# A feed-forward output layer: one 512-column matmul in place of two of 256 columns

## The chip, the cores and the metric

The kernel runs on one core of one Trainium2 chip. The metric is the device time of one execution of the whole program in microseconds (us): two layers of a small model on a sequence of 256 tokens.

## What is computed

The model has two layers. Each layer is a mixer (a state-space branch and an attention branch, merged) and a feed-forward part with a short convolution, and each of them adds its result to the running activations `x`. The change lies in the second matrix product of the feed-forward part:

```python
def conv_ffn(h, w_in, conv_w, conv_b, w_out):
    a, b = jnp.split(h @ w_in, 2, axis=-1)
    a = lax.conv_general_dilated(a, conv_w[:, None, :], window_strides=(1,),
                                 padding=[(CONV_WIDTH - 1, 0)], ...) + conv_b
    return (jax.nn.gelu(a) * b) @ w_out

for l in range(DEPTH):                       # 2 layers, 256 tokens, D_MODEL 1024, D_FF 2816
    x = x + hybrid_mixer(rmsnorm(x, norm_mix[l]), ...)
    x = x + conv_ffn(rmsnorm(x, norm_ffn[l]), ...)
return rmsnorm(x, norm_final)
```

All of it is float32 in the reference.

## The kernel before

Activations lie transposed, features on the 128 partitions and the 256 tokens (`T`) along the free dimension. `w_out` is then 8 output blocks `m` of 128 features, each the sum of 22 products `k` (`KD` = 8, `NF` = 22), so 176 products a layer.

Most products are done in three matmuls, so that the fast matmul type fp32r keeps float32 accuracy. A weight chunk of 1024 columns (8 tiles of 128x128) is loaded into a ring of five `raw` buffers (L147, DMAs on the SP queue). `split` (L154) makes two parts of it: ScalarE casts `raw` to the high part `wh` (L158) and VectorE subtracts it for the low part `wl` (L160); `wh` and `wl` have three buffers each, so a cast waits until TensorE has used the chunk three before. The activations are split in the same way, into `fh` and `fl` here (`split_act`, L163). `mm3` (L167) then issues wh·fh, wh·fl and wl·fh (L169, L170, L171), 256 columns each, all into the first half of one PSUM bank; every matmul loads its own 128x128 weights first (PEld in the profile).

In the output loop of `ffn` (from L944) a block `m` takes a bank `ps_fo` of the two banks with the tag `mm`, runs its 22 products and is then added to `x` by VectorE (`tt`, an addition that the profile shows as L204). Block m+2 needs the bank of block m, and so waits for that addition. Each chunk holds 8 products and is split just ahead of its use, whatever block it falls into: chunk `fo5` is products 40 to 47, `fo6` begins with product 48. In layer 0 the loop also prepares layer 1: after some blocks further chunks are loaded and split (`pre`, L182), and the matrix C of the state-space branch is scaled (`ctmp`, `Cm`).

Nobody writes the order of the instructions by hand in this stage. The program is built with a scheduler that simulates a time line (L1174) and puts every engine's instructions in the order in which that simulation finds them ready; only some rows of TensorE in the mixers are kept together (L175). A changed instruction can therefore move others far behind it. Names in the profile that the text uses: `ps_g` are gate products in the mixer, `pr` and `z` the state-space branch's element-wise products and scans, `rt` and `sw` the rotary embedding, `kk` the compressed keys, `ps_n`, `sq`, `xo` and `ps_x` the final normalization and transposition.

## Time and profile before

| | before |
|---|---|
| median of 3 runs | 856.54 us (854.37 to 856.77) |
| the profiled execution, its own time | 856.18 us |
| its span, first to last instruction | 854.4 us |
| TensorE busy | 813.5 us (95%) |
| VectorE busy | 677.5 us (79%) |
| ScalarE busy | 418.4 us (49%) |
| mean granted TensorE clock | 0.977 |

All times within the execution are counted from the start of the span. The output loop of layer 0 lies at 372 to 434 us, that of layer 1 at 783 to 844 us. The busy time of TensorE counts overlapping matmuls once; a matmul that is listed with 0.28 us can begin 0.11 us after the one ahead of it. For the cost of one matmul, read the distance of the starts.

### The profile page before, as it was taken

How to read it: one execution, taken by the hardware profiler on the slowest of the kernel's cores; microseconds unless marked ns; L12 is line 12 of the kernel's file. 1: busy time of each engine (PE TensorE's matmuls, PEld its weight loads, DVE VectorE, ACT ScalarE, POOL GpSimd, SP SyncE). 2: the span in 40 equal slices, each digit the busy share in tenths (PEclk: the TensorE clock that was granted, in tenths of full speed). 3: DMA queues.
4: the chain of work that ended last, by engine and by line, in shares of the span. 5: the costliest groups of instructions: out<-in, count | busy, mean ns of one | idle time of the engine just before them, and what ended most of it. 6: DMA issues, size and time to landing. Idle time of an engine off the chain costs nothing.

```text
span 854.4 us, 16283 instructions
## 1 busy us (share of the span) xinstructions
PE 813.5 (95%) x6432; PEld 738.4 (86%) x6432; DVE 677.5 (79%) x1277; ACT 418.4 (49%) x786; POOL 23.0 (3%) x56
## 2 busy tenths in 40 slices
PE   8997999999989999999989769999999999999996
PEld 7875786669989999999989657877799999999996
DVE  7979886747998988877666998988588888888553
ACT  3011244664544766656533126667546556655442
POOL 0000000000000000000001110100000000000000
PEclk9998989999999999999999979999999999999998
DMA  7545722625655666667753563234356566555641
GB/s 290 163 117 167 266 75 78 188 80 154 185 158 170 197 198 192 192 185 233 261 173 110 166 221 121 75 92 153 102 173 192 179 195 199 191 195 188 196 147 50
DMA packets 41772, 142.42 MB, mean 167 GB/s; under 512 B 5216, under 2 KB 6752, under 8 KB 41696
## 3 DMA queue, kind: packets, MB, share of 16 engines
q1 hardware_dynamic: 39712, 139.15, 51.1%
q10 hardware_dynamic: 1984, 2.24, 0.9%
q8 instruction: 50, 0.82, 0.4%
q14 instruction: 26, 0.21, 0.1%
HBM read 136.39 MB, written 2.10 MB: 162 GB/s over the span
## 4 chain that ended last, share of the span: by engine, by line
PE 75%; DVE 14%; DMA 5%; issue 3%; ACT 1%; POOL 0%; DVEq 0%; ACTq 0%; SPq 0%
PE ps_f L170 9%; PE ps_f L169 9%; PE ps_f L171 9%; PE ps_g L425 4%; PE ps_fo L171 3%; PE ps_fo L170 3%; PE ps_fo L169 3%; DMA raw<-wst 2%; DVE z L586 2%; PE ps_g L171 2%; PE ps_g L170 2%; PE ps_g L169 2%; PE psy L621 2%; DVE pr L204 2%; PE ps_br L169 2%
## 5 line engine op out<-in xcount | busy, mean ns | idle before, releaser
L158 ACT CAST wh<-raw 128x1024 fp32r<-128x1024 f32 (+1 forms) x199 | 207.6, 1046 | 225.4 <-PE ps_f L170 96.9
L160 DVE TENSOR_TENSOR wl<-raw,wh 128x1024 fp32r<-128x1024 f32 (+1 forms) x199 | 243.8, 1227 | 68.1 <-ACT wh L158 65.1
L170 PE MATMUL ps_f<-al,wh 128*128 128x256 f32 x704 | 195.2, 277 | 2.4 <-DVE al L213 2.4
L169 PE MATMUL ps_f<-ah,wh 128*128 128x256 f32 x704 | 195.3, 278 | 1.2 <-DVE x L213 1.2
L171 PE MATMUL ps_f<-ah,wl 128*128 128x256 f32 x704 | 194.9, 277 | 0.0
L170 PEld LDWEIGHTS ps_f<-al,wh 128*128 128x128 f32 x704 | 132.9, 189 | 2.6 <-DVE al L213 2.6
L169 PEld LDWEIGHTS ps_f<-ah,wh 128*128 128x128 f32 x704 | 132.9, 189 | 1.3 <-ACT wh L158 1.3
L171 PEld LDWEIGHTS ps_f<-ah,wl 128*128 128x128 f32 x704 | 132.8, 189 | 0.0
L171 PE MATMUL ps_fo<-fh,wl 128*128 128x256 f32 x352 | 96.9, 276 | 1.1 <-DVE wl L160 1.1
L170 PE MATMUL ps_fo<-fl,wh 128*128 128x256 f32 x352 | 97.0, 276 | 0.0
L169 PE MATMUL ps_fo<-fh,wh 128*128 128x256 f32 x352 | 96.9, 276 | 0.0
L171 PEld LDWEIGHTS ps_fo<-fh,wl 128*128 128x128 f32 x352 | 65.9, 188 | 1.3 <-DVE wl L160 1.3
L169 PEld LDWEIGHTS ps_fo<-fh,wh 128*128 128x128 f32 x352 | 66.1, 188 | 0.0
L170 PEld LDWEIGHTS ps_fo<-fl,wh 128*128 128x128 f32 x352 | 66.1, 188 | 0.0
L425 PE MATMUL ps_g<-xg,raw 128*128 128x256 f32 x256 | 64.2, 401 | 2.0 <-DMA raw<-wst 1.1
L425 PEld LDWEIGHTS ps_g<-xg,raw 128*128 128x128 f32 x256 | 49.0, 200 | 13.2 <-issue 4.1
L204 DVE TENSOR_TENSOR pr<-z,E 128x512 f32<-128x512 f32 x64 | 43.2, 720 | 8.5 <-PE psy L621 8.5
L169 PE MATMUL ps_g<-ah,wh 128*128 128x256 f32 x128 | 40.0, 312 | 4.4 <-ACT wh L158 4.4
L213 DVE SCALAR_TENSOR_TENSOR cv<-ab,sp,cv 128x255 f32<-128x255 f32 (+1 forms) x88 | 42.0, 480 | 1.7 <-ACT cv L926 0.4
L171 PE MATMUL ps_g<-ah,wl 128*128 128x256 f32 x128 | 39.7, 310 | 3.4 <-DVE wl L160 3.3
L586 DVE TENSOR_TENSOR_SCAN z<-rm,z 128x512 f32<-128x512 f32 x32 | 37.7, 1210 | 2.7 <-POOL z L204 2.7
L170 PE MATMUL ps_g<-al,wh 128*128 128x256 f32 x128 | 39.5, 308 | 0.0
(261 smaller groups left out, 1676.9 us busy)
## 6 DMA issues: line engine op xcount, KB each, us to landing
raw<-wst SPq DMA_DIRECT2D x246, 512.0 KB, 4.2
x<-xT SPq DMA_DIRECT2D x4, 512.0 KB, 4.9
raw<-wst SPq DMA_DIRECT2D x4, 420.0 KB, 3.6
B<-wst SPq DMA_DIRECT2D x2, 512.0 KB, 6.2
xd<-x SPq DMA_DIRECT2D x2, 512.0 KB, 6.6
x<-xd SPq DMA_DIRECT2D x2, 512.0 KB, 5.8
sw<-rt SPq DMA_DIRECT2D x12, 64.0 KB, 3.6
sw<-rt ACTq DMA_DIRECT2D x12, 64.0 KB, 3.8
```

What stands on the lines that cost most here:

```text
L158: S.copy(h[:, :n], t[:, :n])
L160: V.tensor_tensor(lo[:, :n], t[:, :n], h.bitcast(F32)[:, :n], op=OP.subtract)
L169: PE.matmul(ps, wh, ah, start=start, stop=False, **k)
L170: PE.matmul(ps, wh, al, start=False, stop=False, **k)
L171: PE.matmul(ps, wl, ah, start=False, stop=stop, **k)
L204: return e.tensor_tensor(o, a, b, op=op)
L213: e.scalar_tensor_tensor(o, a, s, b, op0=op0, op1=op1)
L425: PE.matmul(ps, w[:, k * 128:(k + 1) * 128], xg[:, k, :], start=k == 0, stop=k == KD - 1, skip_group_check=True)
L586: V.tensor_tensor_scan(f, rt.rearrange("p a t -> p (a t)"), f, 0.0, op0=OP.mult, op1=OP.add)
L621: PE.matmul(psy[32 * a:32 * a + 32, :T], Cm[:, ci, 4 * q + a, :], prs[a // 2][:, a % 2].rearrange("p c t -> p (c t)"), start=(i == 0), sto ...
```

## The change

`fh` and `fl` become the two halves of one tile `f2`, at the same addresses. The matmuls wh·fh and wh·fl become one matmul of 512 columns (L952 of the changed kernel) that writes both halves of the bank: the first half is the sum of the high parts, the second that of the low parts. The third matmul, wl·fh (L953), goes into the first half as before. Each block therefore needs two additions to `x` instead of one. Over both layers 1056 weight loads and matmuls become 704, and 16 additions of 128x256 are new.

```diff
--- before.py
+++ after.py
@@ -914,8 +914,7 @@
 
     def ffn(l, nm, mp):
         ah, al, x = nm.ah, nm.al, nm.x
-        fh = mp.tile([128, NF, T], F32R, name="fh")
-        fl = mp.tile([128, NF, T], F32R, name="fl")
+        f2 = mp.tile([128, 2, NF, T], F32R, name="f2")
         cw = [sp(l, f"cw{i}") for i in range(3)]
         cb = sp(l, "cb")
 
@@ -928,7 +927,7 @@
             stt(cv[:, 2:], ab[:, 0, :T - 2], cw[0][:, i:i + 1], cv[:, 2:], OP.mult, OP.add)
             S.activation(cv, cv, AF.Gelu_apprx_tanh)
             tt(cv, cv, ab[:, 1, :], OP.mult)
-            split_act(fh[:, i, :], fl[:, i, :], cv)
+            split_act(f2[:, 0, i, :], f2[:, 1, i, :], cv)
 
         for i in range(NF):
             ps = bank("ps_f", "mm" if i % 2 == 0 else "aux").rearrange("p (a t) -> p a t", a=2)
@@ -949,8 +948,11 @@
                 if t % 8 == 0:
                     c = split(l, f"fo{t // 8}")
                 wh, wl = wt(c, t % 8)
-                mm3(ps[:, :T], wh, wl, fh[:, k, :], fl[:, k, :], k == 0, k == NF - 1)
+
+                PE.matmul(ps, wh, f2[:, :, k, :], start=k == 0, stop=k == NF - 1, skip_group_check=True)
+                PE.matmul(ps[:, :T], wl, f2[:, 0, k, :], start=False, stop=k == NF - 1, skip_group_check=True)
             ix = tt(x[:, m, :], ps[:, :T], x[:, m, :], OP.add)
+            tt(x[:, m, :], ps[:, T:], x[:, m, :], OP.add)
             if m == 0:
                 first_out = ix
             if l + 1 < L:
```

The order of the instructions moves at three places that matter below. The first is TensorE in layer 1, at the last product (k = 21) of block m = 0; `ps_fo_9316` (before) and `ps_fo_9146` (after) are the bank of m = 0, `ps_fo_9405` and `ps_fo_9214` that of m = 1, and `wh_9379`/`wh_9193` is chunk `fo2`. Before:

```order
L170 MATMUL ps_fo_9405<-fl_7725,wh_9414 128x256
L171 MATMUL ps_fo_9405<-fh_7724,wl_9416 128x256
L169 MATMUL ps_fo_9405<-fh_7724,wh_9414 128x256
L170 MATMUL ps_fo_9316<-fl_7725,wh_9379 128x256
L171 MATMUL ps_fo_9316<-fh_7724,wl_9381 128x256
L170 MATMUL ps_fo_9405<-fl_7725,wh_9414 128x256
L171 MATMUL ps_fo_9405<-fh_7724,wl_9416 128x256
```

And with the change:

```order
L952 MATMUL ps_fo_9214<-f2_7555,wh_9243 128x512
L953 MATMUL ps_fo_9214<-f2_7555,wl_9245 128x256
L952 MATMUL ps_fo_9214<-f2_7555,wh_9243 128x512
L952 MATMUL ps_fo_9146<-f2_7555,wh_9193 128x512
L953 MATMUL ps_fo_9146<-f2_7555,wl_9195 128x256
L953 MATMUL ps_fo_9214<-f2_7555,wl_9245 128x256
L952 MATMUL ps_fo_9214<-f2_7555,wh_9243 128x512
```

The product's matmul with the low activations has to wait for VectorE's last `fl` (`f2`) split and is put into block m = 1. Before, its high half ran earlier and its other two matmuls stand behind 92 matmuls of the loop, some 31 products; now all of it stands behind 67 matmuls, 34 of 512 columns and 33 of 256. Layer 0 has the same rows.

The second place is VectorE there, from the last `fl` split on. `wl_9476`/`wl_9267` is the low part of chunk `fo5`, `wl_9512`/`wl_9296` of `fo6`. Before:

```order
L160 TENSOR_TENSOR wl_9446<-raw_9442,wh_9444 128x1024
L165 TENSOR_TENSOR fl_7725<-cv_9307,fh_7724 128x256
L204 TENSOR_TENSOR x_7420<-ps_fo_9316,x_7420 128x256
L160 TENSOR_TENSOR wl_9476<-raw_9472,wh_9474 128x1024
L160 TENSOR_TENSOR wl_9512<-raw_9508,wh_9510 128x1024
L160 TENSOR_TENSOR wl_9542<-raw_9538,wh_9540 128x1024
L204 TENSOR_TENSOR x_7420<-ps_fo_9405,x_7420 128x256
```

And with the change:

```order
L165 TENSOR_TENSOR f2_7555<-cv_9137,f2_7555 128x256
L160 TENSOR_TENSOR wl_9267<-raw_9263,wh_9265 128x1024
L204 TENSOR_TENSOR x_7251<-ps_fo_9146,x_7251 128x256
L160 TENSOR_TENSOR wl_9296<-raw_9292,wh_9294 128x1024
L204 TENSOR_TENSOR x_7251<-ps_fo_9146,x_7251 128x256
L160 TENSOR_TENSOR wl_9318<-raw_9314,wh_9316 128x1024
L204 TENSOR_TENSOR x_7251<-ps_fo_9214,x_7251 128x256 x2
```

The addition of block 0 stood ahead of the split of `fo5`. Now its first half stands behind that split, and its second half behind the split of `fo6` as well.

The third place is VectorE in the mixer of layer 1, which the diff doesn't touch. `wl_5742`/`wl_5573` and `wl_5901`/`wl_5732` are the low parts of two weight chunks for `ps_g`. Before:

```order
L586 SCALAR_TENSOR_TENSOR z_5330<-rm_5327,z_5330 128x512 x2
L204 TENSOR_TENSOR pr_5966<-z_5330,E_4228 128x512
L204 TENSOR_TENSOR pr_5968<-z_5330,E_4228 128x512
L204 TENSOR_TENSOR pr_5977<-z_5330,E_4228 128x512
L204 TENSOR_TENSOR pr_5979<-z_5330,E_4228 128x512
L204 TENSOR_TENSOR rt_5348<-rt_5348,rc_5041 128x512
L160 TENSOR_TENSOR wl_5901<-raw_5897,wh_5899 128x1024
L165 TENSOR_TENSOR y_5689<-yg_5687,y_5689 128x256
L204 TENSOR_TENSOR rt_5348<-rt_5348,sw_5410 128x512
```

And with the change:

```order
L586 SCALAR_TENSOR_TENSOR z_5161<-rm_5158,z_5161 128x512 x2
L204 TENSOR_TENSOR rt_5179<-rt_5179,rc_4872 128x512
L165 TENSOR_TENSOR y_5520<-yg_5518,y_5520 128x256
L204 TENSOR_TENSOR rt_5179<-rt_5179,sw_5241 128x512
L586 SCALAR_TENSOR_TENSOR z_5161<-rm_5158,z_5161 128x512 x2
L160 TENSOR_TENSOR wl_5732<-raw_5728,wh_5730 128x1024
L204 TENSOR_TENSOR pr_5797<-z_5161,E_4206 128x512
L204 TENSOR_TENSOR pr_5799<-z_5161,E_4206 128x512
L165 TENSOR_TENSOR q_4935<-rt_5179,q_4935 128x512
L204 TENSOR_TENSOR pr_5808<-z_5161,E_4206 128x512
L204 TENSOR_TENSOR pr_5810<-z_5161,E_4206 128x512
```

The split `wl_5901` stood behind four `pr` products and one `rt` step; now it stands ahead of the four products, and behind a second `rt` step and one `y` step that followed it before. A few rows ahead of these, four other `pr` products and the two `kk` products have moved ahead of the first split, `wl_5742`. From VectorE's next `th` step on the order is almost that of before.

## Rows read from the trace of the kernel before

**Rows 1.** The profile page: span, and busy time, share and instructions of each engine.

```profile
span 854.4 us, 16283 instructions
...
PE 813.5 (95%) x6432; PEld 738.4 (86%) x6432; DVE 677.5 (79%) x1277; ACT 418.4 (49%) x786; POOL 23.0 (3%) x56
```

**Rows 2.** Stages: window, length, then busy us of PE, PEld, DVE, ACT, POOL; PEclk, DMA.

```profile
372.00:434.00 62.00, 60.90 (x536) 60.71 (x536) 45.50 (x64) 33.62 (x48) 0.00 (x0) 1.00 0.71 230
...
540.00:550.00 10.00, 10.00 (x69) 8.58 (x67) 10.00 (x21) 5.48 (x16) 2.66 (x6) 0.83 0.17 54
783.00:844.00 61.00, 61.00 (x541) 61.00 (x540) 32.51 (x42) 27.55 (x38) 0.00 (x0) 1.00 0.44 142
```

**Rows 3.** Timeline of PE, layer 1: start us, us, engine, line, operation, count.

```profile
783.66 0.28 PE L169 MATMUL ps_fo<-fh,wh 128*128 128x256 f32 x1
...
794.31 0.28 PE L170 MATMUL ps_fo<-fl,wh 128*128 128x256 f32 x1
```

**Rows 4.** Timeline of all engines at the end of layer 1 and of the program.

```profile
843.39 0.28 PE L171 MATMUL ps_fo<-fh,wl 128*128 128x256 f32 x1
...
843.70 0.42 DVE L204 TENSOR_TENSOR x<-ps_fo,x 128x256 f32<-128x256 f32 x1 [5.59 <-PE ps_fo L171]
...
844.22 0.42 ACT L367 ACTIVATE sq<-x 128x256 f32<-128x256 f32 x1 [6.66 <-DVE x L204]
844.54 0.49 ACT L972 ACTIVATE xo<-x,sp 128x256 f32<-128x256 f32 x1
845.32 0.53 PEld L387 LDWEIGHTS ps_n<-ones,sq 128*128 128x128 f32 x4
...
845.68 0.29 PEld L1003 LDWEIGHTS ps_x<-cc,xo 128*128 128x128 f32 x2
```

**Rows 5.** Timeline of PE: the two-pass matmuls of an early stage.

```profile
23.68 6.42 PE L425 MATMUL ps_q<-xg,raw 128*128 128x256 f32 x29
29.94 1.24 PE L425 MATMUL ps_kc<-xg,raw 128*128 128x256 f32 x5
```

**Rows 6.** Timeline of PE: single-pass matmuls of 280 columns.

```profile
487.83 0.29 PE L171 MATMUL ps_v<-wh,al 128*128 128x280 f32 x1
...
488.23 0.29 PE L171 MATMUL ps_v<-wh,al 128*128 128x280 f32 x1
```

**Rows 7.** Timeline of ACT, layer 1, after the first output block.

```profile
794.40 2.00 ACT L158 CAST wh<-raw 128x1024 fp32r<-128x1024 f32 x2 [3.86 <-PE ps_fo L170]
```

**Rows 8.** Timeline of DVE, layer 1, at the same place.

```profile
794.51 0.42 DVE L204 TENSOR_TENSOR x<-ps_fo,x 128x256 f32<-128x256 f32 x1 [2.68 <-PE ps_fo L171]
795.48 2.37 DVE L160 TENSOR_TENSOR wl<-raw,wh 128x1024 fp32r<-128x1024 f32 x2 [0.55 <-ACT wh L158]
```

**Rows 9.** The chain that ended last, layer 0: start us, us, what.

```profile
388.45 1.06 ACT wh L158
...
393.94 4.81 DMA raw<-wst
...
402.15 6.34 DMA raw<-wst
...
427.93 0.39 PE ps_fo L171
```

**Rows 10.** Timeline of DVE in the mixer of layer 1.

```profile
502.90 3.96 DVE L204 TENSOR_TENSOR pr<-z,E 128x512 f32<-128x512 f32 x4
506.78 0.68 DVE L204 TENSOR_TENSOR rt<-rt,rc 128x512 f32<-128x512 f32 x1
507.39 1.21 DVE L160 TENSOR_TENSOR wl<-raw,wh 128x1024 fp32r<-128x1024 f32 x1
508.52 0.41 DVE L165 TENSOR_TENSOR y<-yg,y 128x256 fp32r<-128x256 f32 x1
508.86 0.68 DVE L204 TENSOR_TENSOR rt<-rt,sw 128x512 f32<-128x512 f32 x1
```

**Rows 11.** Timeline of PE at the same place.

```profile
508.65 0.58 PE L171 MATMUL ps_g<-ah,wl 128*128 128x256 f32 x1 [3.33 <-DVE wl L160]
```

## Prediction

> **What bounds the kernel now.** I read the page first: TensorE (PE) is busy for 813.5 of 854.4 us [rows 1], so the first guess is that every nanosecond taken from a matmul shortens the program. Busy time doesn't say that PE sets the end everywhere, so I read the two changed stages apart [rows 2]. Layer 1's output loop is PE alone: 61.00 of 61 us, with VectorE (DVE) at 32.51. Layer 0's loop looks almost the same, 60.90 of 62, but the chain that ended last leaves PE there: from the cast at 388.45 to the matmul at 427.93 it runs over casts, splits and the weight transfers of 4.81 and 6.34 us and others like them [rows 9]. What PE saves inside that stretch is waited away at its end. Third, I looked outside the stages: the scheduler has reordered the mixer of layer 1, and there PE waits 3.33 us for one weight split [rows 11].
>
> **The matmuls.** The 528 matmuls of layer 1's loop start from 783.66 to 843.39 [rows 3, 4]: 59.73 us over 527 distances, 0.1133 us each, 0.340 for a product of three. The change puts one 512-column matmul for two of 256. No row shows one of this type with all 128 rows, so I bound it. Below: the L425 matmuls are done in two passes, which stream 512 columns for one weight load, and 29 of them start within 6.26 us (23.68 to 29.94), 0.216 each [rows 5]. Above: fp32r matmuls of 280 columns start 0.133 apart (three distances from 487.83 to 488.23 [rows 6]), 0.476 ns a column, and 512 columns at that rate are 0.244. I take 0.216, since that row streams the same number of columns behind the same 128x128 load; the 280-column row has an odd width. A product is then 0.216 + 0.113 = 0.329, 0.011 less than 0.340; at the upper bound it is 0.357, 0.017 more. Over 176 products that is -1.9 us, or +3.0.
>
> The rule against this gain stands in the Trainium skill, "TensorE: Matmul & The Clock Gate", section "Back-to-back issue gap": a warm isolated matmul costs N/2.4 + 2.5 ns, so 216 ns for 512 columns but 109 for 256. By it a product would go from 327.5 to 325 ns and layer 1 would gain 0.4 us instead of 1.9, with 855.1 us in all instead of 853.6. On 512 columns the trace agrees with the page (0.216), on 256 it measures 113 and not 109, and the measurement decides.
>
> **Two new waits at the first block's end.** The last product of block 0 now stands as a whole behind 34 matmuls of 512 and 33 of 256 columns: 34 x 0.216 + 33 x 0.113 = 11.07 us, against 92 x 0.1133 = 10.42 before, so 0.65 later. On it hangs the buffer for chunk fo5. Before, its L170 started at 794.31 [rows 3], the cast of fo5 began at 794.40 and two casts took 2.00 [rows 7], and the two splits began at 795.48 and took 2.37, 1.18 each [rows 8]. Now the cast begins at about 795.15 (0.65, and 0.1 for the longer matmul), fo5's split at 796.23, and it ends at 797.41. PE reaches the first matmul on that split 40 x 0.216 + 39 x 0.113 = 13.05 us into the loop, 2.63 after the 10.42 of L170, at 796.94: it waits 0.5. Behind that on DVE stand the first addition of block 0 (0.42 [rows 8]), fo6's split (1.18) and the second addition (0.42): 799.3 to 799.4. Block 2 wants that bank after one more matmul and three products, at 798.5: it waits 0.8. Before, neither wait was there, because the addition stood ahead of both splits. In layer 1 nothing hides these 1.3 us, so its loop comes to -1.9 + 1.3 = **-0.6 us**.
>
> **Layer 0.** The same rows stand there, so block 2 begins 5.0 us after the place of that L170. The cast at 388.45, with which the chain leaves PE [rows 9], needs the last use of chunk fo5, three products later: 5.0 + 3 x 0.329 + 0.1 = 6.1 us after L170, against 50 x 0.1133 = 5.7 before. The chain thus starts 0.4 later and everything on it up to 427.93 with it; what PE gains meanwhile only makes its wait there longer. The 16 products after 427.93 give back 16 x 0.011 = 0.2. Layer 0: **+0.2 us**. Bounds: -0.4 if the new waits don't come, +1.9 with the 0.244 matmul.
>
> **The 16 additions** are 16 x 0.42 = 6.7 us on DVE, in stages where it has 16.5 and 28.5 us idle [rows 2]; apart from the one above they lie beside matmuls. At the end of the program one follows the last matmul. Before, sq ended at 844.22 + 0.42 = 844.64, while PE's load for ps_n began at 845.32 behind the transpositions, and xo ended at 845.03 against 845.68 [rows 4]. 0.42 more on either still comes before PE: **0 us**. If the transpositions were not there it would cost 0.42.
>
> **The mixer of layer 1.** The split that PE waits for until 508.65 [rows 11] started at 507.39, behind four pr products that hold DVE from 502.90 to 506.78 [rows 10]. In the changed order it stands ahead of them (-3.88) and behind a y step (0.34) and an rt step (0.60, both by their distance to the next start [rows 10]): 2.9 us earlier. What could stop that: its cast needs a transfer that is now queued behind two small sw transfers on SP, but these are released earlier too, because the kk products moved forward. The four pr products before the first split delay that one by some 2 us, into a time when PE idles anyhow. From 508.65 on the chain runs over PE nearly without a break to the end of the program, so an earlier start lasts, unless DVE, which is busy for 10.00 of 10 us at 540 to 550 [rows 2], becomes the bound. GpSimd's rotary product now meets scans instead of pr products and may slow those. Bounds: -2.9 and 0, or a loss if the pr products, now later, are waited for; they end about 1 us later than before, but the matmuls that read them stand far behind. I take **-2.5 us**, near the worked value.
>
> **Sum.** -0.6 + 0.2 + 0 - 2.5 = -2.9 us. The profiled execution took 856.18 (span 854.4), so 853.3; it lies 0.36 below the median of 856.54, on whose scale I forecast **853.6 us**. About 0.3%, 2.6 us, is what a measurement of this kernel can tell from no change, so "faster" means below 854.0.
>
> **Rivals.**
> The first: the mixer gains nothing, since DVE or a weight transfer takes the place of the split as the bound. For it speaks DVE's full window, against it the 3.33 us wait on a single split. -0.6 + 0.2 = -0.4: 856.1 us, no change that can be measured. Chance 0.30.
>
> The second ends slower: the 512-column matmul costs 0.244. The place is the two output loops; the price is +3.0 + 1.1 (the same waits) in layer 1 and +1.9 in layer 0, and with the mixer's -2.5 it is +3.5: 860.0 us. It decides from about 0.24 on, where the loops lose more than the mixer gives. The 280-column row speaks for it, the two-pass row against it. Chance 0.13.
>
> The third: the second 256 columns cost next to nothing, because the load of the weights and not the stream paces the matmuls. A product would be 2 x 0.113 = 0.227 and layer 1 would gain 176 x 0.113 = 20 us, while layer 0 stays with its transfers: about 836 us. The 0.216 of the two-pass row, with one load for 512 streamed columns, speaks against it. Chance 0.02. The same section of the Trainium skill names 131 ns as sustained spacing at N = 512, which would be near this; no row of this trace shows it.
>
> The fourth: the change takes the place of matmuls but the two new waits don't arise, because the scheduler's rows leave more room than I count; then layer 1 gives -1.9 and layer 0 -0.4, and with the mixer's -2.5 it is 851.7 us. Chance 0.12.
>
> **How the numbers follow.** The forecast has 0.43: 853.6, by itself 852.3 to 855. Faster by over 0.3%: 0.26 of it (the mixer's and the matmul's terms decide), the third and fourth rival, and 0.04 at the low edge of the first: 0.44. Slower: the second rival, and 0.04 of the first if the later pr products are waited for, 0.17. Within 0.3%: the rest, 0.39. The range 851.0 to 857.5 takes in the fourth rival and most of the first, and leaves out the second, the third and the edges, some 0.18.
>
> **What would show it.** In the changed profile: starts of L952 and L953 that are 0.216 and 0.113 apart and 0.329 a product in layer 1; a wait of 0.5 for wl and one of 0.8 for an addition to x some 13 to 16 us into each output loop; in layer 0 the cast of 388.45 later by 0.4, and at its end a longer wait of PE for a split; ps_n at the end behind the transpositions as before; and in the mixer the wait of 3.3 us for wl at 508.65 gone or ended near 505.8. I am wrong if a product takes over 0.34, if that mixer wait only changes its place, or if the clock differs between the runs by more than the terms.

## The result: 0.9% slower

| | median | lowest to highest | profiled span | mean granted clock |
|---|---|---|---|---|
| before | 856.07 us (5 runs) | 854.37 to 856.77 | 854.4 us | 0.977 |
| after | 862.63 us (5 runs) | 861.28 to 866.62 | 861.0 us | 0.973 |

The ratio is 1.0088, with a 95% interval of 1.0061 to 1.0116. The forecast was 853.6 us with a range of 851.0 to 857.5: wrong in sign, and the result lies outside the range.

The head of the profile after answers [rows 1]: 352 matmuls and as many weight loads fewer and 16 VectorE instructions more, as the diff says, yet TensorE (PE) is busy for longer.

```profile
span 861.0 us, 15595 instructions
...
PE 817.5 (95%) x6080; PEld 727.3 (84%) x6080; DVE 683.7 (79%) x1293; ACT 419.0 (49%) x786; POOL 23.6 (3%) x56
```

I laid the two traces side by side at the same places (by the starts of the first and last matmul of a stage; us):

| | before | after | difference |
|---|---|---|---|
| first `ps_fo` matmul of layer 0 | 372.04 | 372.15 | +0.1 |
| length of layer 0's output loop | 61.97 | 62.03 | +0.1 |
| from the end of that loop to the first `ps_wo` matmul (the mixer of layer 1) | 206.2 | 210.4 | **+4.2** |
| first `ps_wo` to the first `ps_fo` of layer 1 | 143.4 | 143.4 | 0.0 |
| length of layer 1's output loop | 59.73 | 62.03 | **+2.3** |
| last `ps_fo` to the last `ps_x` | 2.55 | 2.56 | 0.0 |

These lengths, like every stage length below, come from one execution of each kernel. Thirteen kernels here with the same instruction order up to layer 0's output loop begin it anywhere from 369.6 to 374.4 us, so a stage can differ by some us between executions alone.

So the loss of 6.6 us has two places: the loop that was rewritten, and a stage that the diff doesn't touch.

**The loop.** The timeline of PE at the head of layer 1's loop after (start us, us, engine, line, operation, count) answers [rows 3]:

```profile
789.03 0.40 PE L952 MATMUL ps_fo<-f,wh 128*128 128x512 f32 x1
789.26 0.28 PE L953 MATMUL ps_fo<-f,wl 128*128 128x256 f32 x1
789.38 0.40 PE L952 MATMUL ps_fo<-f,wh 128*128 128x512 f32 x1
789.62 0.28 PE L953 MATMUL ps_fo<-f,wl 128*128 128x256 f32 x1
```

The second column is how long one is in the engine; what costs is the distance of the starts. From L952 to the next it is 0.233 us over the loop, from L953 0.120: a product costs 0.353 where three matmuls cost 0.340. There is no wait in it; 176 times 0.013 are the 2.3 us. About half of the 13 ns lies on the 512-column matmul (233 against twice 113) and half on the 256-column one behind it (120 against 113).

**The mixer.** What PE waited for between 480 and 600 us, after (waits: what for, us in total, times, longest):

```profile
PE ps_g L171 <- DVE wl L160: 5.3, 1, 5.3
PE ps_g L169 <- ACT wh L158: 3.8, 2, 2.9
PE ps_g L169 <- DVE th L204: 2.4, 2, 1.8
```

The wait for the split, which was to shrink, grew from 3.3 us [rows 11] to 5.3, and the one for `th` is new. VectorE (DVE) after, where [rows 10] showed four `pr` products:

```profile
501.92 0.69 DVE L204 TENSOR_TENSOR rt<-rt,rc 128x512 f32<-128x512 f32 x1 [1.60 <-DMA sw<-rt]
502.52 1.50 DVE L165 TENSOR_TENSOR y<-yg,y 128x256 fp32r<-128x256 f32 x1
503.94 0.69 DVE L204 TENSOR_TENSOR rt<-rt,sw 128x512 f32<-128x512 f32 x1
505.29 2.34 DVE L586 TENSOR_TENSOR_SCAN z<-rm,z 128x512 f32<-128x512 f32 x2 [0.66 <-POOL z L204]
507.55 1.20 DVE L160 TENSOR_TENSOR wl<-raw,wh 128x1024 fp32r<-128x1024 f32 x1
...
513.26 2.34 DVE L160 TENSOR_TENSOR wl<-raw,wh 128x1024 fp32r<-128x1024 f32 x2
515.53 0.68 DVE L204 TENSOR_TENSOR th<-ps_g,rb 128x512 f32<-128x512 f32 x1
```

The split does stand ahead of the `pr` products now, but it starts at 507.55, where it started at 507.39 before: the two scans ahead of it start 4.6 us later than before (505.29 against 500.64), and the `th` step behind it 1.8 us later (515.53 against 513.75). The first `ps_s` matmul is then 2.2 us late, counted from the end of layer 0's loop, and the last one 4.2 us. The chain that ended last, after, between 492 and 512 us (start us, us, what), shows what the scans waited for:

```profile
495.95 5.84 DMA sw<-rt
...
502.04 1.70 POOL sw L204
503.74 0.96 POOL cy L204 x2
```

The rotary transfers `sw<-rt` are issued 3.1 us earlier than before (from 495.36 on, against 498.49), but the last of them is on the way for 5.84 us and lands at 501.79, where before it landed at 501.38. GpSimd (POOL) has its multiply ahead of the carry `cy` that the scans need; before, the carry came first, and the scans had no transfer to wait for (POOL, then DVE, before):

```profile
499.67 0.37 POOL L204 TENSOR_TENSOR cy<-z,pw 128x8 f32<-128x8 f32 x2 [18.02 <-DVE z L586]
...
504.00 1.71 POOL L204 TENSOR_TENSOR sw<-sw,rc 128x512 f32<-128x512 f32 x1
...
500.64 2.34 DVE L586 TENSOR_TENSOR_SCAN z<-rm,z 128x512 f32<-128x512 f32 x2 [0.43 <-POOL z L204]
```

At 552.67 PE waits a second time, 1.8 us for a `th` step, and works at the lower clock level behind it (granted clock 0.50, which is 1.2 GHz; starts 0.213 apart instead of 0.113), up to 558.6:

```profile
552.67 0.58 PE L169 MATMUL ps_g<-ah,wh 128*128 128x256 f32 x1 [1.82 <-DVE th L204]
...
553.90 0.41 PE L171 MATMUL ps_g<-ah,wl 128*128 128x256 f32 x1
554.12 0.41 PE L169 MATMUL ps_g<-ah,wh 128*128 128x256 f32 x1
```

Before, the clock was at that level here too, without a wait, from 544.9 to 548.3: for 17 matmuls instead of 28. At 0.1 us each the difference is worth about 1.1 us by this estimate. No run takes it out by itself; in loads_held below the clock stands at 1.00 from 540 to 560, and its mixer is no shorter (211.9 us).

### The profile page after: what moved, and what is told of

Read it like the earlier page. It is cut to its first block, busy times and chain, and to the rows that moved or that the text cites. A ratio compares the mean times of both kernels' runs of the same rounds, so it can differ in the third digit from the quotient of the medians.

```text
span 861.0 us, 15595 instructions
## 1 busy us (share of the span) xinstructions
PE 817.5 (95%) x6080; PEld 727.3 (84%) x6080; DVE 683.7 (79%) x1293; ACT 419.0 (49%) x786; POOL 23.6 (3%) x56
## 4 chain that ended last, share of the span: by engine, by line
PE 81%; DVE 10%; DMA 4%; issue 3%; ACT 1%; POOL 1%; DVEq 0%; ACTq 0%; SPq 0%; POOLq 0%
PE ps_fo L952 10%; PE ps_f L170 9%; PE ps_f L169 9%; PE ps_f L171 9%; PE ps_fo L953 5%; PE ps_g L425 5%; PE psy L621 2%; DMA sw<-rt 2%; PE ps_g L169 2%; PE ps_g L171 2%; PE ps_g L170 2%; PE ps_s L756 2%; PE ps_br L169 2%; PE ps_br L171 2%; PE ps_br L170 2%
## 5 line engine op out<-in xcount | busy, mean ns | idle before, releaser
L160 DVE TENSOR_TENSOR wl<-raw,wh 128x1024 fp32r<-128x1024 f32 (+1 forms) x199 | 242.7, 1221 | 70.3 <-ACT wh L158 69.4
L952 PE MATMUL ps_fo<-f,wh 128*128 128x512 f32 x352 | 124.2, 397 | 0.0
L953 PE MATMUL ps_fo<-f,wl 128*128 128x256 f32 x352 | 99.3, 283 | 0.0
L952 PEld LDWEIGHTS ps_fo<-f,wh 128*128 128x128 f32 x352 | 66.4, 189 | 15.3
L953 PEld LDWEIGHTS ps_fo<-f,wl 128*128 128x128 f32 x352 | 66.5, 189 | 0.2
L169 PE MATMUL ps_wo<-mt,wh 128*128 128x256 f32 x128 | 35.4, 279 | 0.6 <-DVE x L213 0.6
L170 PE MATMUL ps_wo<-mt,wh 128*128 128x256 f32 x128 | 35.3, 276 | 0.0
```

Source lines behind the costliest of these rows:

```text
L160: V.tensor_tensor(lo[:, :n], t[:, :n], h.bitcast(F32)[:, :n], op=OP.subtract)
L169: PE.matmul(ps, wh, ah, start=start, stop=False, **k)
L170: PE.matmul(ps, wh, al, start=False, stop=False, **k)
L952: PE.matmul(ps, wh, f2[:, :, k, :], start=k == 0, stop=k == NF - 1, skip_group_check=True)
L953: PE.matmul(ps[:, :T], wl, f2[:, 0, k, :], start=False, stop=k == NF - 1, skip_group_check=True)
```

## Experiments

"Mixer" below is always the third line of the table above: 206.2 us before, 210.4 after.

### One layer at a time

**only_layer1**: the change in layer 1 alone.

```diff
+        wide = l == 1
...
-                mm3(ps[:, :T], wh, wl, fh[:, k, :], fl[:, k, :], k == 0, k == NF - 1)
+                if not wide:
+                    mm3(ps[:, :T], wh, wl, f2[:, 0, k, :], f2[:, 1, k, :], k == 0, k == NF - 1)
+                    continue
```

> The change in layer 1 alone; layer 0 keeps its three matmuls (its activations lie in one tile as in the changed kernel). My theory is that the loss has two sources: 2.3 us from the output loop of layer 1, whose product takes 0.353 instead of 0.340 us, and 4.3 us from the mixer of layer 1, which the scheduler orders otherwise because layer 0 changed. Then this kernel keeps the mixer as before (PE's wait for wl near 508.65 stays 3.3, ps_s ends at 572.9) and loses only the loop: about 856.1 + 2.3 = 858.4 us. The rival, that both losses come from the wider matmul and the 16 additions wherever they stand, gives half of the whole difference: about 859.4, with part of it outside the loop of layer 1.

Measured 857.44 us, ratio 1.0039 (1.0017 to 1.0060). Its layer 1 loop takes 62.03 us, its mixer 205.9. The loop loses 2.3 us by itself, and the mixer loses nothing where layer 0 is left as it was.

**only_layer0**: the other half.

```diff
+        wide = l == 0
```

> The change in layer 0 alone. My theory: the output loop of layer 0 itself ends where it did (434, it waits for transfers at its end anyhow), GpSimd's sw multiply again stands ahead of the carry of the scan, and the mixer of layer 1 loses its 4.3 us, the loop of layer 1 nothing: about 860.4 us, ps_s ends near 577.2. The rival, that the mixer loses because of its own chance timing in that one run and not through the order, gives a mixer as before and 856 us.

Measured 859.27 us, 1.0060 (1.0038 to 1.0082). Layer 1's loop is 59.73 us as before, the mixer 211.6: it is the change in layer 0 that costs the mixer its time, without a product of layer 1 being touched.

### What paces a 512-column matmul

**forms**: each of the eight blocks of layer 1 with products of another form.

```diff
+                elif form == 2:
+                    j = min(k, NF - 2)
+                    PE.matmul(ps, wh, f2[:, 0, j:j + 2, :], start=k == 0, stop=last, **q)
...
+                elif form == 3:
+                    PE.matmul(ps, wh, two, start=k == 0, stop=last, **q)
+                    PE.matmul(ps[:, :T], wh, one, start=False, stop=last, **q)
+                elif form == 4:
+                    PE.matmul(ps, wh, two, start=k == 0, stop=last, **q)
+                    PE.matmul(ps, wl, two, start=False, stop=last, **q)
```

> Layer 0 as before. In layer 1 each of the eight output blocks takes another form of the product, and part of the sums are not the reference's: blocks 0, 1 and 7 as in the change (512 columns in two pieces by wh, 256 by wl); 2: the 512 columns are one contiguous piece; 3: the 256-column matmul takes wh as well; 4: 512 columns in two pieces by wh and again by wl; 5: three of 256, weights wh, wl, wh; 6: three of 256 as before, wh, wh, wl. Read is the distance of the starts. If the two pieces cost the 17 ns (the stream has to jump), block 2 has 0.216 and 0.113 and block 4 0.233 each. If the change of weights from matmul to matmul costs it (before, every second load was of the same tile), block 3 has 0.216 and 0.113 and block 5 shows 0.120 and not 0.113. If 512 columns cost it as such, blocks 2, 3 and 4 all show 0.233, and blocks 5 and 6 both 0.113.

This kernel and the three that follow ran once each; the figures are medians over the products of a block, 22 or a few less. Distance from a matmul's start to the next, in ns: two pieces 233 and 120 (512 and 256 columns), one contiguous piece of 512 234 and 120, the same weights for both 235 and 119, two of 512 229 and 233, 256 columns with changing weights 113 to 114. So neither the two pieces of the operand nor the change of weights costs the 17 ns over 216.

**shift**: the activations begin 32 m bytes further on in block m.

```diff
+        fx = mp.tile([128, 2 * NF * T + 64], F32R, name="f2")
...
+                    g2 = shifted(8 * m)
+                    PE.matmul(ps, wh, g2[:, :, k, :], start=k == 0, stop=k == NF - 1, skip_group_check=True)
```

> Layer 0 as before; layer 1 has the two matmuls of the change, but block m reads the activations 32 x m bytes further on (0 to 224 bytes; the sums are then not the reference's). Weights and activations both stream out of SBUF at the same time, and the kernel has small pads between its pools that set how their addresses stand to each other. If a collision of the two streams costs the extra 17 and 7 ns, the distances differ between the blocks, with 0.216 and 0.113 at some shift and perhaps more than 0.233 at another. If addresses don't matter, all blocks show 0.233 and 0.120.

228 to 234 and 116 to 120 ns, the least (228 and 118) at 96 to 160 bytes. The address is worth 6 ns at most; 216 is never seen.

**widths**: two matmuls of one width in each product.

```diff
+                    n1, n2, mw = [(512, 512, 128), (384, 384, 128), (320, 320, 128), (256, 256, 128),
+                                  (192, 192, 128), (512, 512, 64), (256, 256, 64), (512, 256, 64)][m]
...
+                    PE.matmul(ps[:mw, :n1], wh[:, :mw], fx[:, a:a + n1], start=k == 0, stop=last, skip_group_check=True)
```

> A measurement of the rates; the sums are not the reference's. Layer 1: two matmuls a product, by wh and by wl, and in each block one width from one contiguous piece: 512, 384, 320, 256, 192 columns with all 128 weight columns; then 512, 256 and the pair 512 and 256 with 64 weight columns. Layer 0: three matmuls of 256 as before, block m reading 32 x m bytes further on. If a matmul costs a fixed part and then 1/2.4 ns a column, 512 to 320 lie on one line from 113 at 256 with 107 ns more at 512 (0.220). If the columns run slower as such (0.443 ns each), 384 takes 170, 320 takes 142 and 512 takes 227. If the weights that load meanwhile take cycles from the stream, the blocks with 64 weight columns are faster than those with 128: 512 goes towards 216, 256 towards 109. The shift in layer 0 shows whether 0.113 itself depends on the addresses.

192 columns 111 to 113 ns, 256 113 to 114, 320 142 to 147, 384 176 to 177, 512 229 to 233. With half the weight columns 512 take 230 to 232 and 256 117 to 119. From 320 on this is about 0.45 ns a column with no fixed part, and narrower weights make it no faster: from 256 columns on there is no cost of a matmul that a wider one would save. Two rows of the 384-column block (timeline of PE):

```profile
801.12 0.34 PE L965 MATMUL ps_fo<-f,wh 128*128 128x384 f32 x1
801.29 0.34 PE L966 MATMUL ps_fo<-f,wl 128*128 128x384 f32 x1
```

**types**: plain float32, bf16 and fp32r (the kernel's type here) in the same loop.

```diff
+                        PE.matmul(ps[:, :n], w.bitcast(F32), fx[:, a:a + n].bitcast(F32), start=w is wh and k == 0,
+                                  stop=w is wl and last, **q)
...
+                        PE.matmul(ps[:, :n], identb if w is wh else bt[:, :128], bt[:, :n],
+                                  start=w is wh and k == 0, stop=w is wl and last, **q)
```

> A measurement of rates; the sums are not the reference's. Layer 0 as before; in layer 1 two matmuls a product in each block: 0 and 1 plain float32 (two passes) of 256 and of 512 columns; 2 and 3 bf16 of 512 and 256 columns; 4 fp32r of 512 columns that lie 128 bytes further on; 5 fp32r of 512, always the same weight tile; 6 fp32r of 512 that go to two PSUM banks in turn; 7 three of 256 as before, but wh by fl into the second half of the bank. My prediction took 0.216 for 512 columns from a two-pass float32 row. If the type makes the difference, block 1 takes 0.432 and block 2 0.216, and 4 to 6 stay at 0.23. If 512 columns are slow in every type, block 1 takes about 0.46 and block 2 0.23. If the bank is the cause, block 6 is faster than 0.23 and block 7 slower than 0.113.

This decides it. Timeline of PE in that kernel, first plain float32 of 256 columns (two records for one matmul), then bf16 of 512, then fp32r of 512:

```profile
785.56 0.59 PE L963 MATMUL ps_fo<-f,wh 128*128 128x256 f32 x2
785.99 0.59 PE L963 MATMUL ps_fo<-f,wl 128*128 128x256 f32 x2
...
844.05 0.38 PE L968 MATMUL ps_fo<-bt,identb 128*128 128x512 bf16 x1
844.26 0.38 PE L968 MATMUL ps_fo<-bt 128*128 128x512 bf16 x1
...
860.33 0.39 PE L973 MATMUL ps_fo<-f,wh 128*128 128x512 f32 x1
860.56 0.39 PE L973 MATMUL ps_fo<-f,wl 128*128 128x512 f32 x1
```

A pass of plain float32 takes 0.216 for 256 columns (0.43 for the two) and 0.429 for 512, bf16 of 512 columns takes 0.216 and of 256 0.109, and fp32r of 512 0.229 to 0.233. The stream is slower by type, 0.45 ns a column in fp32r against 0.42 in bf16. The fp32r blocks that lie 128 bytes further on, use one weight tile or go to two banks all stay at 229 to 233 ns, and three of 256 with the second half of the bank at 113 to 114. Why the 256-column matmul behind one of 512 takes 120 is not shown: the rate alone would give 115, and it stayed at 116 to 120 in every form and at every address tried.

### The mixer: the order of its instructions

**split_first**, on the kernel before: only the move that the prediction counted on, two of the four `pr` products put behind the split.

```diff
+                    late = l == 1 and q == 1 and h == 0 and i >= 1
+                    with tc.issue_after(low[1, "g9"].ins) if late else nullcontext():
```

> The kernel before, where only two of the four pr products that stand ahead of the split at 507.39 are issued behind it. This is the mixer term of my prediction without the rest of the reordering. If TensorE's wait there was for that split alone, the split starts some 2.0 us earlier, the wait at 508.65 ends near 506.7, and the program takes 2.0 us less than the kernel before. If a transfer, the cast or VectorE further on takes its place, it takes as long as before.

856.53 us, 1.0012 (0.9991 to 1.0033): no change. The split starts 2.2 us earlier (505.15), the first `th` too (511.5), but the last of the five `th` steps stands at 576.3 in both, and the mixer takes 206.7. The waits of PE in it (480 to 600 us; lines are numbered two higher) show the place:

```profile
PE ps_g L173 <- DVE wl L162: 3.7, 1, 3.7
PE ps_g L171 <- DVE th L206: 2.2, 2, 1.8
```

What PE gains at the split it waits for DVE's `th` steps 40 us later; before, it had no wait for them.

**sw_held**, on the kernel after: the rotary multiply behind the carry, the `rt` steps behind the second scans.

```diff
+    def p_qd():
+        with tc.issue_after(carry[1].ins), tc.issue_after(scans[7].ins):
+            for f in held:
+                f()
```

> The changed kernel in both layers, and in the mixer of layer 1 the tail of one rotary step is issued later: GpSimd's sw multiply behind the carry of the scan (as it stood before the change), VectorE's two rt steps behind the second pair of scans. My theory: the 4.3 us were lost because the sw multiply, ahead of the carry in GpSimd's queue, waits for a DMA until 502.0, and the second scans, the split and TensorE wait behind it. Then the second scans start near 500.7 again and not at 505.3, the split that TensorE waits for near 505.5 and not at 507.55, and the program takes about 858.4 (only the 2.3 of layer 1's loop are left) or a little less. The rival, that the mixer loses elsewhere (the clock after the longer wait, or the wait for th at 552), leaves 861 to 862.

The edit also brings the carry's own step forward in the written order. A miss: 866.45 us, 1.0112 (1.0088 to 1.0136). The scans did come back to 500.71, the split to 506.21 and the first `ps_s` matmul to 519.7 (522.8 after); but from 520 to 532 the granted clock is 0.57 (0.96 after) and the mixer takes 214.6. Windows of that kernel (length, busy us of PE, PEld, DVE, ACT, POOL, granted clock, DMA share, GB/s):

```profile
508.00:520.00 12.00, 12.00 (x87) 11.56 (x85) 10.50 (x18) 5.45 (x7) 1.29 (x1) 0.78 0.70 209
520.00:532.00 12.00, 12.00 (x54) 8.11 (x52) 8.12 (x22) 5.23 (x18) 0.00 (x0) 0.57 0.15 51
```

**sw_ahead**, on the kernel before: only GpSimd's order of after, the carry behind the rotary multiply.

```diff
+            if l == 1 and q == 1:
+                with tc.issue_after(sws[2].ins):
+                    carry(q, cy, zl, e)
+                return
```

> The kernel before, its output loops untouched; only in the mixer of layer 1 GpSimd gets the order that the change brought: the sw multiply of one rotary step ahead of the carry of the scan (the scheduler then also puts VectorE's rt steps ahead of the second scans, as in the changed kernel). My theory: this order by itself makes the mixer some 2 to 4 us longer, since the carry, the second scans and all behind them on VectorE wait for a DMA; the second scans start near 505 and not at 500.6, and the program takes 858 to 860. The rival: the order at this place doesn't matter, any gain or loss up to 520 is made up by 576, and the 4.3 us come from what the scheduler moved later, at 550 to 560; then it takes 856 within 0.3%.

My theory of the order fell here: 855.35 us, 0.9999 (0.9984 to 1.0015), mixer 206.9, though the second scans start at 503.59, 3.0 later than before. The transfers took 2.0 and 2.3 us in it. In this kernel GpSimd's order and late scans cost nothing; the order of VectorE differs in some 30 to 40 rows from both kernels, so it isn't the order of after alone.

### The mixer: the clock

**fill_before** and **fill_after**: 26 and 42 matmuls on zeros in PE's wait for the split, in the kernel before and in the one after.

```diff
+                        for _ in range(fill):
+                            PE.matmul(ps, zerob, causb.rearrange("p a t -> p (a t)"), start=False, stop=False,
+                                      skip_group_check=True)
```

> The kernel before with 26 matmuls by an all-zero tile (128x256, sums unchanged) behind the two matmuls ahead of TensorE's 3.3 us wait at 505 to 508.6, so that TensorE works instead of waiting. Theory: a good part of the mixer's time is the granted clock, which stands at the lower level (0.50) in the 5.5 us behind that wait and costs some 2.6 us there; then the clock stays at 1.0 and ps_s begins up to 2.6 us earlier. Whether the program gains them depends on what is late next: if VectorE paces the stretch from 500 to 552, as the run with the split moved suggests, the program takes as long as before (856); if TensorE does, 2 us less.

> The changed kernel with 42 such zero matmuls in its longer wait (5.3 us, 503.5 to 508.8). GpSimd's and VectorE's order up to the split stay as in the changed kernel. If the clock carries some 3 of the 4.3 us that the mixer lost, ps_s ends about 3 us earlier than 577.2 and the program takes about 859.5. If the loss is VectorE's start alone, it stays at 862.

fill_before: 859.5 us, 1.0044 (1.0026 to 1.0063), mixer 211.8, with a later order of its own, so it says little. fill_after: 861.27 us, 1.0074 (1.0053 to 1.0094). Its windows show full clock where after has 0.64 (508 to 520) and 0.96 (520 to 532):

```profile
508.00:520.00 12.00, 11.20 (x94) 9.57 (x93) 11.53 (x25) 5.24 (x9) 1.84 (x1) 1.00 0.53 169
520.00:532.00 12.00, 11.45 (x96) 8.72 (x92) 12.00 (x26) 9.38 (x30) 0.00 (x0) 1.00 0.27 85
532.00:545.00 13.00, 12.27 (x92) 9.28 (x93) 13.00 (x20) 5.76 (x15) 4.65 (x6) 0.93 0.18 51
```

Counted from the end of layer 0's loop, `ps_s` starts 4.4 us earlier than after (at 516.5 here), yet the mixer takes 209.5, 0.9 less than after: DVE is busy for every microsecond from 520 to 545. So the half clock behind this first wait doesn't set the mixer's end by itself here. The order behind the split isn't that of after (some 33 of 292 VectorE rows moved), and the lower clock at the second place is still there (0.50 from 543.2 to 549.8).

### The mixer: the transfers

**loads_held**, on the kernel after: four of the five weight loads issued beside the rotary transfers wait until these are used.

```diff
+        if l and nm in ("g2", "g4", "g5", "g12"):
+            tc.add_manual_dep(i.ins, sws[2].ins.name,
```

> The changed kernel, GpSimd's order unchanged (sw multiply ahead of the carry); only four weight loads of layer 1's mixer that SP issues right behind the sw transfers wait until that sw multiply is done. The order alone cost nothing in the run before (there the sw transfers took 2.3 us, since the weight loads came 2.4 us after them; in the changed kernel they take 5.8 us, beside the loads that start 0.7 us after). Theory: it is this meeting of transfers on the DMA engines, together with GpSimd's order, that starts the second scans 4.7 us late. Then the sw transfers take about 3 us, the second scans start near 502.5 and not at 505.3, TensorE's wait of 5.3 us for wl becomes shorter by some 2 us, and the program takes 858.4 to 860. The rival, that the transfers are slow for another reason or that the held loads are then late themselves, leaves it at 862.

A miss too: 864.4 us, 1.0103 (1.0084 to 1.0121); with one load beside it the transfer still takes 5.27 us. Its chain:

```profile
498.07 5.27 DMA sw<-rt
```

So it isn't the number of loads alone. What the slow cases share is in the view of DMA queues: queue q8 moves instructions in packets of 16 KB, and by their number they are PE's: 50 in the program for 6432 matmuls before, 48 for 6080 after. Fewer matmuls in layer 0 shift all later packets, and in after one falls at 496.3, in the middle of the four rotary issues; in loads_held it is at 498.5. After, from 495.3 to 502.5 (queue: packets, MB, share; then issues, KB each, median us to landing):

```profile
q8 instruction: 1, 0.02, 1.0%
...
raw<-wst SPq DMA_DIRECT2D x5, 512.0 KB, 5.8
sw<-rt SPq DMA_DIRECT2D x2, 64.0 KB, 3.1
sw<-rt ACTq DMA_DIRECT2D x2, 64.0 KB, 4.6
```

Before, from 498.4 to 503, no packet of q8 (the nearest is at 491.1):

```profile
raw<-wst SPq DMA_DIRECT2D x4, 512.0 KB, 6.5
sw<-rt SPq DMA_DIRECT2D x2, 64.0 KB, 2.0
sw<-rt ACTq DMA_DIRECT2D x2, 64.0 KB, 2.3
```

The two issues on ScalarE's (ACT) queue, which go out side by side with SP's, take 2.53 us after and 1.46 before (timeline):

```profile
495.36 2.53 ACTq L502 DMA_DIRECT2D sw<-rt  x2
```

```profile
498.49 1.46 ACTq L502 DMA_DIRECT2D sw<-rt  x2
```

The last three kernels move the packets by one-column matmuls at the program's start (and a tile of ones for them). Nothing else is written differently, though the scheduler moves rows again.

**fetch_moved**, on the kernel after, to take the packet away:

```diff
+    for i in range(80):
+        PE.matmul(warm[:, :1], onesb, onesb[:, :1], start=True, stop=True, skip_group_check=True)
```

> The changed kernel with 80 one-column matmuls more at the start of the program, which move every later load of TensorE's instructions (packets of 16 KB, one per 128 matmuls) by 80 matmuls; the order in layer 1's mixer up to the split stays. In all five traces where the sw transfers near 495 take 4 us or more (the changed kernel among them), such a packet begins 0.9 to 1.3 us after their issue; in the five where they take 2.0 to 2.3, it lies 5 to 7 us earlier. Holding back the weight loads didn't make them faster. Theory: the packet stops them for some 2 us, and GpSimd's order passes that on to the scan and the split. Then the packet lies near 486 and 510 here, the sw transfers take about 2.3 us, the second scans start near 502 and not at 505.3, ps_s begins some 2 us earlier relative to the output loop of layer 0, and of the 4.3 us a good part is gone (the start of the program costs some us more). The rival: the packet is there by chance; then the transfers still take 4 to 5 us.

**fetch_onto** and **fetch_onto2**, on the kernel before, to put one there:

```diff
+    for i in range(76):
```

> The kernel before with 76 one-column matmuls more at the start, so that a packet of TensorE's instructions falls on the sw transfers near 497 (the scheduler puts GpSimd's sw multiply ahead of the carry here as well, which cost nothing by itself). Theory of the packet: the sw transfers take 4 to 6 us instead of 2.3, the second scans start near 505, and layer 1's mixer is 2 to 4 us longer than before. The rival: they take 2.3 as before and the mixer is as long as before.

```diff
+    for i in range(103):
```

> As the run before with 103 instead of 76 one-column matmuls at the start. There the packet of TensorE's instructions began at 501.62, 3.5 us after the issue of the sw transfers, which had landed by then (2.0 and 2.3 us). 27 matmuls more move it to about 1 us behind the issue. Theory of the packet: now the sw transfers take 4 to 6 us, GpSimd's sw multiply and the second scans start 2 us or more later than in that run, relative to the issue. The rival: they take 2.0 to 2.3 again.

The scheduler moved the mixer's instructions here too: fetch_onto, built on the kernel before, has nearly the order of after (six of 292 VectorE rows stand elsewhere, in fetch_moved as well, and the two differ from each other by one). So they compare nearly one order with short and with long transfers. The last column but one is the start of the second pair of scans, counted, like the mixer, from the end of layer 0's loop:

| kernel | order of the mixer | packet among the transfers | transfers on SP / ACT, us | second scans, us | mixer, us |
|---|---|---|---|---|---|
| before | before | no | 2.0 / 2.3 | 66.6 | 206.2 |
| only_layer1, forms, shift | before | no | 2.0 / 2.3 | 65.8, 65.8, 64.7 | 205.9, 206.2, 205.4 |
| widths | before | no | 2.0 / 2.3 | 68.1 | 208.3 |
| after | after | yes | 3.1 / 4.6 | 71.1 | 210.4 |
| only_layer0 | after | yes | 3.2 / 4.8 | 72.9 | 211.6 |
| fetch_moved | nearly after | no | 2.6 / 2.8 | 69.4 | 208.0 |
| fetch_onto | nearly after | no, 3.5 us after the issue | 2.0 / 2.3 | 68.8 | 208.0 |
| fetch_onto2 | another (some 32 rows differ from after) | yes, 0.5 us after the issue | 2.8 / 3.0 | 70.0 | 208.6 |
| split_first | another | no | 2.0 / 2.3 | 66.1 | 206.7 |
| sw_ahead | another | no | 2.0 / 2.3 | 70.4 | 207.0 |
| types | another | no | 2.0 / 2.3 | 67.1 | 209.5 |
| fill_before | another | no | 2.0 / 2.3 | 66.0 | 211.8 |
| fill_after | another | yes | 3.9 / 4.1 | 70.8 | 209.5 |
| loads_held | another | yes | 2.9 / 4.2 | 71.9 | 211.9 |
| sw_held | another | yes | 3.4 / 5.0 | 67.2 | 214.6 |

All three of the last experiments are slower than before, 865.65 us (1.0139, 1.0106 to 1.0172), 862.44 (1.0095, 1.0068 to 1.0121) and 860.75 (1.0084, 1.0066 to 1.0102): layer 0's loop begins 5.6, 4.2 and 3.2 us later than before or after. The added matmuls explain only a part of that (at the first `ps_q` matmul, near 23 us, the three are 0.5, 0.1 and 1.1 us behind); the rest arises later in layer 0, whose rows were moved as well. So their mixers are compared and not their times, and the times don't show the gain: fetch_moved is 4.4 us above after by the ratios, with a loop that begins 5.6 later and intervals of 5 to 6 us in width.

In the nine kernels with the order of before, of after or nearly that of after, the mixer's length follows the second scans: it is 138.6 to 140.7 us longer than their start, whichever order it is. In the other orders the distance varies more (136.6 in sw_ahead to 147.4 in sw_held), and the mixer's length doesn't go by the transfers there (209.5 in types and 211.8 in fill_before with short ones, 209.5 in fill_after with long ones).

In nearly one order, then, the mixer takes 208.0 us with short transfers, twice, and 210.4 and 211.6 with long ones. The late transfers would cost 2.4 to 3.6 us by this, the larger part of the loss. Two things keep that from being proven: the five kernels with the order of before already lie 2.9 us apart, and one of the six moved rows is a `th` step like the one that PE waits for at 552.67 in after (1.8 us; the wait for `th` is 0.6 in fetch_moved).

The other 1.8 us, from 206.2 to 208.0, lie within the spread that widths shows too. What delays the scans in the two kernels with short transfers can be read, though. In fetch_moved (POOL, then DVE) GpSimd's multiply now runs beside the first pair of scans, which takes 3.38 us instead of 2.33 after, and the carry then takes until 509.13, 1.8 us, instead of 0.9 before:

```profile
504.81 1.36 POOL L208 TENSOR_TENSOR sw<-sw,rc 128x512 f32<-128x512 f32 x1 [17.78 <-DMA sw<-rt]
507.33 0.91 POOL L208 TENSOR_TENSOR cy<-z,pw 128x8 f32<-128x8 f32 x2 [1.16 <-DVE z L590]
...
503.87 3.38 DVE L590 TENSOR_TENSOR_SCAN z<-rm,z 128x512 f32<-128x512 f32 x2
...
509.17 2.34 DVE L590 TENSOR_TENSOR_SCAN z<-rm,z 128x512 f32<-128x512 f32 x2 [0.38 <-POOL z L208]
```

Why the transfers take so long in after stays open. fetch_onto2 has the packet among them without the loads, and they take 0.7 to 0.8 us more, not 2 to 3. There the weight loads started only at 500.09, behind late rotary issues, where SP sent its first at 496.67 in after. On ACT's queue the packet alone goes with 0.7 us more (fetch_onto2), the loads alone with 0.5 (fetch_moved), both together with 2.3 (after), and loads_held with a single load is nearly as slow as after (4.2 against 4.6).

## Why the prediction was wrong, point by point

**The product.** The step that failed is "I take 0.216, since that row streams the same number of columns behind the same 128x128 load". It doesn't. [Rows 5] are plain float32, and each of their records is one pass of 256 columns behind a load of its own: the 16 matmuls of a `ps_q` block stand in the trace as 32 records and 32 weight loads, and in types a 256-column float32 matmul takes two records of 0.216, 0.43 in all. So no row of before showed 512 columns in 0.216, and the agreement with the page that the prediction notes for that row was none. [Rows 6], set aside for "an odd width", were of the right type, fp32r: their 0.476 ns a column gave 0.357 a product, and 0.353 was measured. The term was -1.9 and came to +2.3, near the bound of +3.0. I had chosen a row by its shape, and had misread the shape, where the type decides. This is the second rival's mechanism, at a chance of 0.13; that its 860.0 us lies near the measured time is luck, since its waits (+1.1), its loss in layer 0 (+1.9) and its gain in the mixer (-2.5) didn't come.

The rule of the Trainium skill, "TensorE: Matmul & The Clock Gate", section "Back-to-back issue gap", N/2.4 + 2.5 ns, is met to the nanosecond by bf16 (109 and 216). A pass of plain float32 takes what the rule gives for twice its columns (216 at 256, 429 at 512). fp32r departs from it in both widths (113 and 229 to 234), and the 131 ns that the section names for 512 columns was seen in no run.

**The two waits after block 0** (+1.3) didn't come; neither loop of after has a PE wait. The wrong words are "On it hangs the buffer for chunk fo5". The three buffers of the high parts aren't taken in a fixed turn: in after, fo5 has the buffer of fo3, whose last matmul ends near 799.0 (before, it had that of fo2, with block 0's last product in it). Its cast ran at once, at 799.05, and the split after it at 800.13 (DVE, layer 1's loop after):

```profile
800.13 1.23 DVE L160 TENSOR_TENSOR wl<-raw,wh 128x1024 fp32r<-128x1024 f32 x1 [3.78 <-ACT wh L158]
801.27 0.42 DVE L204 TENSOR_TENSOR x<-ps_fo,x 128x256 f32<-128x256 f32 x1
801.60 1.22 DVE L160 TENSOR_TENSOR wl<-raw,wh 128x1024 fp32r<-128x1024 f32 x1
802.74 0.42 DVE L204 TENSOR_TENSOR x<-ps_fo,x 128x256 f32<-128x256 f32 x1
```

fo5's low part is done at 801.36; PE reaches its first matmul on it at about 802.3. It is fo6 that takes the buffer of block 0's last product; its cast at 800.30 (ACT) is released by that matmul, and ACT idles 0.20 us for it:

```profile
800.30 1.05 ACT L158 CAST wh<-raw 128x1024 fp32r<-128x1024 f32 x1 [0.20 <-PE ps_fo L952]
```

The fourth rival was right on this point alone.

**Layer 0** (+0.2): +0.1 between the two traces, but not in the way I told it. The longer wait at the loop's end didn't come: the 1.1 us for which PE waited there before are gone, and the slower products fill the time. That cover is thin. In nine other kernels here with the old layer 0 the loop took 60.6 to 61.1 us, in all but one with the new one 62.03, so up to 1.4 us of loss may be covered by chance in the trace of before.

**The 16 additions and the end**: right. Last `ps_fo` to last `ps_x` is 2.56 against 2.55, and no addition is waited for.

**The mixer** (-2.5) came to +4.2 and was wrong at several steps. The -2.9 counted the rows that the split passed and left the start of the second scans ahead of it where it was; they start 4.6 us later, because GpSimd's carry now stands behind a multiply that waits for the rotary transfers. "GpSimd's rotary product now meets scans" saw that meeting and gave it no price; in fetch_moved the first scans take 1.0 us more beside it. The words "these are released earlier too" took the time of a transfer for its release plus a fixed duration: they were issued 3.1 us earlier and the last landed 0.4 later (501.79 against 501.38). No row of before showed a packet of instructions meeting them, and the place of the packets moves with every matmul taken out. And "an earlier start lasts" is wrong by itself: split_first made the split 2.2 us earlier and nothing arrived at the end, because DVE's `th` steps were late next. I had named that and left it to the first rival, whose zero was right for the move alone.

**The sum**: -0.6 + 0.2 + 0 - 2.5 = -2.9 was forecast; +2.3 + 0.1 + 0 + 4.2 = +6.6 came. The largest error is the mixer's 6.7 us, a term on code that the diff doesn't touch. With that term as forecast the sum would still have come to -0.1, no gain that can be measured. How much of the 4.2 us belongs to the transfers, to the order and to the spread between executions stays open.

**Something better?** No kernel here beats the one before. split_first (1.0012) and sw_ahead (0.9999) equal it.

## What to carry to other kernels

Take the price of a new matmul from rows of its own type, whatever their width, and check how many columns one record covers: in fp32r two matmuls of 256 columns cost no more than one of 512, so joining them saves nothing. A wait that is shortened counts only as far as the next engine's work is early too; look for what is late next before taking the gain to the end of the program. A change in the number of instructions moves every later instruction packet and the order at places that the diff doesn't touch, so terms there deserve a range of both signs.

## What the runs showed of the hardware

- fp32r streams at about 0.45 ns a column from 320 columns on (142 to 147 ns at 320, 176 to 177 at 384, 229 to 234 at 512), where bf16 takes 0.42 (216 ns at 512). At 192 columns it takes 111 to 113 ns, hardly less than the 113 at 256 (widths, types).
- A plain float32 matmul has two records, each 216 ns at 256 columns and 429 at 512 (types).
- The start address of the streamed operand matters by a few ns: three 256-column matmuls a product in the widths kernel are 113 to 114 ns apart at shifts of 0 and 128 bytes and 118 to 121 at the others tried (layer 0). Three of them then cost 0.355 or more, which is above the changed product at any shift tried (0.346 to 0.353), so the 2.3 us hold for the addresses of this kernel.
- With a 16 KB packet of instructions among them the rotary transfers of 64 KB took 2.8 and 3.0 us instead of 2.0 and 2.3 (fetch_onto2 against fetch_onto); with the packet and weight loads one took 5.84 us (after).
- A pair of scans on VectorE took 3.37 and 3.38 us beside a GpSimd multiply (fetch_onto, fetch_moved) and 2.33 without one (after).
